# A decoder block with retrieved experts: two groups of four token tiles instead of three, with three dense tiles' gates made at the end of the second

## The chip, the cores and the metric

One core of a Trainium2 chip runs the whole block in one program. The metric is the device time of an execution in microseconds; a number given for a kernel is the median of its runs. TensorE is PE in the rows (its weight loads PEld), VectorE is DVE, ScalarE ACT, GpSimd POOL, and SyncE, which issues most transfers, SP. All arithmetic is in fp32.

## The reference

1024 tokens of width 1024 pass through one layer: a conditioned norm, a combined input projection (2304 columns), sliding-window attention and a short gated convolution, an output projection, then a retrieval layer that takes most of the time. Its core:

```python
q = (hf @ w_query).reshape(t, 8, 256)                       # 8 heads
s1 = einsum('thd,hnd->thn', q[..., :128], peer_keys1)       # 128 keys a half
s2 = einsum('thd,hnd->thn', q[..., 128:], peer_keys2)
v1, i1 = top_k(s1, 16);  v2, i2 = top_k(s2, 16)
sc, ci = top_k(v1[..., :, None] + v2[..., None, :], 16)     # over the 256 pairs
e1, e2 = i1[ci // 16], i2[ci % 16]
idx, gates = e1 * 128 + e2, softmax(sc)
a   = gelu(einsum('td,thkd->thk', hx, peer_u[idx]))         # peer_u, peer_v: 16384 x 1024
out = einsum('thk,thkd->td', gates * a, peer_v[idx])
```

So each token uses 8 x 16 of 16384 experts. The result is scaled, added to the residual stream and normed.

## The kernel before, in words

**Tiles and their two ways.** The tokens are eight tiles of 128 (0 to 7). For the tiles in `SPARSE` (2, 6, 7) the retrieval is computed with gathers: POOL issues indirect DMAs that fetch one row of U or V for 128 tokens at a time (L939, 256 rows a tile), and DVE multiplies and sums them (L960 for U, L967 for V). `ROWS` = (3, 7) says how many row buffers there are: three ahead of the dense stage and seven in it. For the tiles in `DENSE` (0, 1, 3, 4, 5) it is computed with matmuls over all experts, 128 blocks of 128 experts, weighted by a table of gates that is zero for the experts that a token doesn't use.

**The front stage** handles the tiles in `GROUPS`: [0, 1, 2], [3, 4, 5] and [6, 7]. One `Front.run` does a group: norm, 18 blocks of 128 columns of the input projection, attention and convolution between them, 8 blocks of the output projection, the second norm, 16 blocks of queries. A block is one `lin` (L257): a weight tile of 128 columns is the stationary operand, and the group's tokens, 128 wide a tile, move, so that a matmul is 384 or 256 wide. For precision weights and activations are split into a high half H and a low half L (fp32r), and a block is 24 matmuls: 8 slices of the depth in three products, H·H, H·L and L·H (L264 to L270). `Weights.load` fetches a weight block once for each group and splits it in two parts of four slices: ACT casts H (L223), POOL subtracts to get L (L224). The activations' halves of groups one and two lie in `hDH` and `hDL`, five tiles wide, which the dense stage reads later; a group's second norm writes them over those of the first. Group two starts at the third tile, since tile 2 isn't dense. Group three has its own, `hSH` and `hSL`.

After each query block come the scores against 128 keys (L622), and DVE takes the 16 largest with five instructions a tile (`top16`, L139; MAX8, FIND_INDEX8, MATCH_REPLACE8). Every second block, `pairs_head` (L645) forms the candidates of a head on POOL and takes their 16 largest. The vectors of the conditioning come from w_ada on DVE and PE (L733 to L751) in group one: the first third ahead of its projections, the rest beside them (`extra`). The first norm of a group is made during the queries of the group ahead of it (`after`, `norm_ahead`, `put_all`).

**Selection and gates.** `select` (L664) turns a tile's candidates into gates (softmax, L672 to L678) and two expert numbers a pair. `choose` (L890) does this for a gathered tile and makes its indices. `dense_gates1` (L796) does it for a dense tile and then builds that tile's gate table, four tokens at a time, which I call a quad: one DVE instruction compares the key numbers with the tokens' e1 and e2 (`oh`, 128 x 1024, L813); every third quad's e1 half is multiplied by the gates on ACT (four instructions, L822), the others' on POOL (L826); four PE matmuls give the table 128 x 128 of each token (`G`, L836), and ACT copies them to a staging tile (L837). A staging tile holds `TG` = 32 tokens; with its last quad ACT's queue writes it to `G_d` in DRAM (L839), in runs of `GB` x `TG` floats. There are two staging tiles and three of `oh`.

**What runs beside what.** `Beside` lets a generator advance at a rate per unit of the front stage's work. The gates of tiles 0 and 1 run beside group two and those of 3, 4 and 5 beside group three (`gates_of`), as do the gathers of tile 2 (`gather`). `RATE_G` and `RATE_F` hold the rates, separate for the projections ("p") and the queries ("q"). Ahead of the first norm of group three all gates of 0 and 1 are finished, and a staging tile serves as its buffer (`ahead_of_last`). In the front stage the order of the instructions on each engine is made by a scheduler from the program's order and its own estimates.

**The dense stage** (`dense_experts`, L1052) follows. A block of 128 experts has an A product (L1112; U's halves against the dense tiles' tokens, in two pieces of 384 and 256 columns, `DENSE_CH`), then ACT's gelu on it, DVE's weighing by the table `Gb` (L1129, read from `G_d` for two blocks at a time, L1065), its H (ACT, L1130) and L (DVE, `WL`, L1133). Four blocks make a set, and for each set there are ten V products (L1158; 12 matmuls of 512 columns each). The stage starts with four A products; then two or three V products alternate with one A. U and V are split beside it: `split_U` (ACT L1075, POOL L1079, with two buffers for `UL`) and `split_V` (ACT L1091, POOL L1095). Here the order on each engine is the program's own (`manual_schedule`):

```python
seq = [("A", b) for b in range(CB)]
for k in range(nk):
    vu = [("V", k, hf, t) for hf in range(2) for t in range(ND)]
    for q in range(CB):
        if k + 1 < nk:
            seq.append(("A", (k + 1) * CB + q))
        seq += vu[q * 2 * ND // CB : (q + 1) * 2 * ND // CB]
```

What is left of the gathers is spread over the stage, and the selections of tiles 6 and 7 (`chosen`) are put between its first steps (L1304).

Of the kernel before, what the change touches and what calls it, by code (L numbers as in the profile page):

```python
# [18 lines left out]
P = 128  # L19
# [12 lines left out]
SPARSE = [2, 6, 7]  # L32
DENSE = [0, 1, 3, 4, 5]
DENSE_CH = [(0, 3), (3, 2)]
GROUPS = [[0, 1, 2], [3, 4, 5], [6, 7]]
ND = len(DENSE)
WD = ND * P
TG = 32
# [46 lines left out]
def block_kernel(  # L85
# [31 lines left out]
    hDH = cst.tile([P, NC, WD], F32R, name="hDH")  # L117
    hDL = cst.tile([P, NC, WD], F32R, name="hDL")
# [34 lines left out]
    with ExitStack() as fctx:  # L153
# [82 lines left out]
        def fp_small(name):  # L236
            return cst.tile([P, 48], F32, tag="hc", name=name)

        class Front:
# [225 lines left out]
            def run(self, prev=0, extra=None, modulate1=None, after=None):  # L465
# [42 lines left out]
                for cb in range(4):  # L508
                    for kind in range(3):
                        blk = 6 + 3 * cb + kind  # L510
                        at = 3 * cb + kind
                        if nxt < n and at % 3 == 0:
                            pend = (nxt, self.att_scores(nxt, qo))
                            nxt += 1
# [27 lines left out]
                        if pend is not None and at % 3 == 2:  # L542
# [63 lines left out]
                for hs in range(16):  # L606
# [24 lines left out]
                    for j, i in enumerate(self.tiles):  # L631
                        if hs == 0:
                            tb[i] = sl_.tile([P, 2, 16, 8], BF16, tag="tb", name=f"tb{i}", bufs=ND)
# [11 lines left out]
        def pairs_head(i, h, tv):  # L645
# [3 lines left out]
            if h == 0:  # L649
                scv[i] = sl_.tile([P, 8, 16], F32, tag="scv", name=f"scv{i}", bufs=ND)  # L650
                ci[i] = sl_.tile([P, 8, 16], U32, tag="ci", name=f"ci{i}", bufs=ND)
# [112 lines left out]
        def ada_rest(fp, n):  # L764
# [6 lines left out]
            elif n in (6, 7):  # L771
                r = fp.tile([P, 512], F32, tag="adar", name=f"adar{n}", bufs=2)
                ada_row(fp, n, acc, r)
                nc.sync.dma_start(s2_d[:, hs], r[0:1, :])
            elif n in (8, 9):
                r = fp.tile([P, 512], F32, tag="adar", name=f"adar{n}", bufs=2)
# [9 lines left out]
            elif n >= 10:  # L786
                r = fp.tile([P, 512], F32, tag="adar", name=f"adar{n}", bufs=2)
# [4 lines left out]
        def dense_gates(gg, tiles):  # L792
            for i in tiles:
                yield from dense_gates1(gg, i)

        def dense_gates1(gg, i):  # L796
# [10 lines left out]
            for tg in range(P // TG):  # L807
                stg = gg.tile([P, NK, TG], F32, tag="stg", name=f"stg{i}_{tg}", bufs=2)
                for q in range(TG // 4):
# [10 lines left out]
                    if q % 3 == 2:  # L820
# [159 lines left out]
        def front(q, hH, hL):  # L980
# [3 lines left out]
            front(0, hDH[:, :, 0 : 3 * P], hDL[:, :, 0 : 3 * P]),  # L984
            front(1, hDH[:, :, 2 * P :], hDL[:, :, 2 * P :]),
# [6 lines left out]
        with tc.tile_pool(name="f0", bufs=1) as f0:  # L992
# [4 lines left out]
            hT = f0.tile([P, NC, P], F32, name="hT0")  # L997
# [16 lines left out]
        gates_of = Beside(dense_gates(gg, [0, 1]))  # L1014
        last = Front(GROUPS[2], [(0, 2)], None, None, "g2")

# [371 lines left out]
```

## Time and profile before

| | |
|---|---|
| median of 3 runs | 2893.73 us (2891.33 to 2896.70) |
| profiled execution | 2898.18 us, its span 2896.4 us |
| mean granted clock of PE in it | 0.96 |
| busy in the span | PE 92%, DVE 77%, POOL 66%, ACT 36% |
| chain that ended last | PE 60%: A (L1112) 28%, V (L1158) 27% |
| first V product of the dense stage | at 1122.78 us |

A span is one profiled execution from its first to its last instruction. Busy shares are averages over stages with different limits, so a change in one stage is judged by that stage's own rows. In the rows below a number behind "x" counts instructions, L is the line of the program that issued them, and what stands in square brackets or behind the last bar is the engine's idle time and the work that ended it.

### The profile page before, as it was taken

What the parts mean: (1) busy time and instruction counts of PE and PEld (TensorE: products, weight loads), DVE (VectorE), ACT (ScalarE), POOL (GpSimd) and SP (SyncE); (2) the same over time, 40 slices, a digit from 0 to 9 for tenths busy, and PEclk for the clock granted to TensorE, in tenths of its full rate; (3) what the DMA queues carried; (4) which work ended last, traced back from release to release, by engine and by line L of the source; (5) the groups of instructions that cost most, each with busy time, mean ns of one, the idle gap of its engine ahead of it and who ended that gap; (6) DMA issues with size and microseconds to landing.
All of it is one profiled execution on the core that took longest, in us unless ns stands there. A gap on an engine that the chain in (4) does not pass through costs nothing.

```text
span 2896.4 us, 44035 instructions
## 1 busy us (share of the span) xinstructions
PE 2676.4 (92%) x15358; PEld 2430.8 (84%) x15358; DVE 2234.3 (77%) x4693; ACT 1034.7 (36%) x2219; POOL 1907.0 (66%) x1894
## 2 busy tenths in 40 slices
PE   5999877998789887999999999999999999999997
PEld 4778776788668786999999889999999899999996
DVE  8835998659977787787777777777778777777776
ACT  3345445474356642222222322222222222222222
POOL 2435755557646665777777677777777777777771
PEclk9999888799899998999999999999999999999999
DMA  8535357674356856988989899988988898898884
GB/s 315 207 92 173 92 142 220 186 191 123 93 119 172 224 163 213 336 303 335 342 317 336 300 332 331 336 326 314 338 317 335 307 341 327 315 338 319 322 326 147
DMA packets 381979, 750.63 MB, mean 259 GB/s; under 512 B 188598, under 2 KB 194742, under 8 KB 381756
## 3 DMA queue, kind: packets, MB, share of 16 engines
q0 software_dynamic: 110592, 402.70, 37.8%
q1 hardware_dynamic: 107004, 303.16, 30.4%
q10 hardware_dynamic: 164160, 41.94, 6.7%
q8 instruction: 121, 1.98, 0.3%
q14 instruction: 102, 0.84, 0.1%
HBM read 695.79 MB, written 51.92 MB: 258 GB/s over the span
## 4 chain that ended last, share of the span: by engine, by line
PE 60%; DVE 4%; POOL 3%; issue 3%; DMA 1%; ACT 1%; another core or an unknown queue 0%; SPq 0%; POOLq 0%; DVEq 0%; ACTq 0%
PE A L1112 28%; PE V L1158 27%; PE G L836 2%; DVE oh L813 1%; POOL VL L1095 1%; PE lin_g2in L267 1%; POOL L L224 1%; PE lin_g2o L267 1%; POOL u L939 1%; PE lin_g2q L267 1%; POOL oh L826 0%; DMA xr<-x1d 0%; DMA raw<-in_w_query_dram 0%; POOL UL L1079 0%
## 5 line engine op out<-in xcount | busy, mean ns | idle before, releaser
L224 POOL TENSOR_TENSOR L<-raw,H 128x512 fp32r<-128x512 f32 x252 | 336.1, 1344 | 287.7 <-ACT H L223 200.2
L939 POOL DMA_INDIRECT u<-in_peer_u_dram,idx x384 | 364.9, 950 | 240.3 <-DVE u L960 93.6
L1158 PE MATMUL V<-VH,WH 128*128 128x512 f32 x1280 | 502.9, 393 | 14.2 <-DVE acc_d L1165 10.4
L939 POOL DMA_INDIRECT v<-in_peer_v_dram,idx x384 | 362.2, 943 | 211.1 <-DVE u L960 69.0
L1158 PE MATMUL V<-VH,WL 128*128 128x512 f32 x1280 | 500.7, 391 | 0.0
L967 DVE SCALAR_TENSOR_TENSOR acc<-v,wv,acc 128x1024 f32<-128x1024 f32 x381 | 489.5, 1285 | 13.5 <-DMA v<-in_peer_v_dram,idx 9.1
L1158 PE MATMUL V<-VL,WH 128*128 128x512 f32 x1280 | 499.1, 390 | 0.0
L960 DVE SCALAR_TENSOR_TENSOR u<-u,h 128x1024 f32<-128x1024 f32 x384 | 457.5, 1214 | 6.9 <-DMA u<-in_peer_u_dram,idx 4.3
L1117 ACT ACTIVATE A<-A 128x384 f32<-128x384 f32 (+1 forms) x256 | 107.7, 422 | 972.8 <-PE A L1112 777.2
L1112 PE MATMUL A<-hDH,UH 128*128 128x384 f32 (+1 forms) x2048 | 344.8, 311 | 19.2 <-ACT UH L1075 18.2
L1095 POOL TENSOR_TENSOR VL<-V,VH 128x512 fp32r<-128x512 f32 x256 | 331.6, 1308 | 35.1 <-ACT VH L1091 32.7
L1112 PE MATMUL A<-hDH,UL 128*128 128x384 f32 (+1 forms) x2048 | 340.3, 308 | 7.4 <-POOL UL L1079 7.4
L1112 PEld LDWEIGHTS A<-hDH,UH 128*128 128x128 f32 x2048 | 321.5, 190 | 30.0 <-ACT UH L1075 19.0
L1129 DVE TENSOR_TENSOR A<-A,Gb 128x384 f32<-128x384 f32 (+1 forms) x256 | 126.3, 497 | 280.5 <-ACT A L1117 213.8
L1112 PE MATMUL A<-hDL,UH 128*128 128x384 f32 (+1 forms) x2048 | 341.4, 309 | 0.0
L1079 POOL TENSOR_TENSOR UL<-U,UH 128x1024 fp32r<-128x1024 f32 x128 | 309.1, 2415 | 31.6 <-ACT UH L1075 29.3
L1112 PEld LDWEIGHTS A<-hDH,UL 128*128 128x128 f32 x2048 | 308.6, 188 | 8.6 <-POOL UL L1079 8.6
L1112 PEld LDWEIGHTS A<-hDL,UH 128*128 128x128 f32 x2048 | 311.3, 189 | 0.0
L1158 PEld LDWEIGHTS V<-VH,WH 128*128 128x128 f32 x1280 | 241.1, 188 | 64.3 <-DVE acc_d L1165 15.1
L1158 PEld LDWEIGHTS V<-VH,WL 128*128 128x128 f32 x1280 | 240.9, 188 | 52.5
L1158 PEld LDWEIGHTS V<-VL,WH 128*128 128x128 f32 x1280 | 241.4, 189 | 46.1
L1165 DVE TENSOR_TENSOR acc_d<-acc_d,V 128x512 f32<-128x512 f32 x310 | 211.8, 683 | 57.1 <-PE V L1158 53.1
(311 smaller groups left out, 4335.5 us busy)
## 6 DMA issues: line engine op xcount, KB each, us to landing
U<-in_peer_uT_dram SPq DMA_DIRECT2D x128, 512.0 KB
V<-in_peer_v_dram SPq DMA_DIRECT2D x256, 256.0 KB
G_d<-stg ACTq DMA_DIRECT2D x20, 2048.0 KB
Gb<-G_d SPq DMA_DIRECT2D x64, 640.0 KB
raw<-in_w_in_dram SPq DMA_DIRECT2D x54, 512.0 KB
wada<-in_w_ada_dram SPq DMA_DIRECT2D x48, 512.0 KB
raw<-in_w_query_dram SPq DMA_DIRECT2D x48, 512.0 KB
raw<-in_w_out_dram SPq DMA_DIRECT2D x24, 512.0 KB
```

Source lines behind the costliest of these rows:

```text
L224: nc.gpsimd.tensor_tensor(L, src, H.bitcast(F32), op=ALU.subtract)
L267: nc.tensor.matmul(ps[:, :w], wt[:, c, :], h[:, q * (NC // 2) + c, o : o + w], start=(k == 0), stop=(k == 3 * NC - 1),)
L939: nc.gpsimd.indirect_dma_start(out=t, out_offset=None, in_=peer_u if which == "u" else peer_v, in_offset=bass.IndirectOffsetOnAxis(ap=idx[ ...
L960: nc.vector.scalar_tensor_tensor(t, t, 1.0, h2[i], op0=ALU.mult, op1=ALU.mult, accum_out=av[i][:, j : j + 1])
L967: nc.vector.scalar_tensor_tensor(acc[i], t, wv[i][:, j : j + 1], acc[i], op0=ALU.mult, op1=ALU.add)
L1079: nc.gpsimd.tensor_tensor(L, Ur.pop(b), Up[b][0].bitcast(F32), op=ALU.subtract)
L1095: nc.gpsimd.tensor_tensor(L, Vr.pop(v), Vp[v][0].bitcast(F32), op=ALU.subtract)
L1112: nc.tensor.matmul(ps[:, : n * P], u[:, c, :], h[:, c, sl], start=(k == 0), stop=(k == 3 * NC - 1))
L1117: nc.scalar.activation(w, w, AF.Gelu)
L1129: nc.vector.tensor_tensor(w3, w3, g, op=ALU.mult)
L1158: nc.tensor.matmul(ps, w[:, ts_], v, start=(n == 0), stop=(n == 3 * CB - 1))
L1165: nc.vector.tensor_tensor(accs[0][:, t, hs], accs[0][:, t, hs], ps, op=ALU.add)
```

## The change

- Two groups: `GROUPS` = [0, 1, 2, 3] and [4, 5, 6, 7]. A projection matmul is 512 wide; each weight block is loaded and split twice, not three times. Group three, with its buffers and its staging-tile norm, goes.
- `SPARSE` is now 2, 3, 7 and `DENSE` 0, 1, 4, 5, 6, still three and five. `hDH` and `hDL` are six tiles wide, group two starts at the third (`SECOND` = 2), and the first norm of its first two tiles waits in `hT0`, which is two tiles wide.
- Attention of a tile is put at every second block of the input projection instead of every third.
- The gates of tiles 0 and 1 run beside group two, as before, followed by the selection of tile 3. The gates of tiles 4, 5 and 6 are written behind group two, with all multiplications by the gates on POOL (`beside` is False).
- Only tile 7's selection is left between the first steps of the dense stage.
- `TG` is 16: a staging tile has half the tokens, and a write to `G_d` has 2 x 16 floats a run in place of 2 x 32.
- Buffers: w_ada 4 instead of 6, the conditioning rows 1 instead of 2, `UL` 1 instead of 2, gather rows in the dense stage 6 instead of 7.

```diff
-SPARSE = [2, 6, 7]
-DENSE = [0, 1, 3, 4, 5]
+SPARSE = [2, 3, 7]
+DENSE = [0, 1, 4, 5, 6]
-GROUPS = [[0, 1, 2], [3, 4, 5], [6, 7]]
+GROUPS = [[0, 1, 2, 3], [4, 5, 6, 7]]
+SECOND = 2
-TG = 32
+TG = 16
-ROWS = (3, 7)
+ROWS = (3, 6)
-RATE_F = {("p", 1): 0.3, ("q", 1): 0.0, ("p", 2): 0.1, ("q", 2): 0.0}
-RATE_G = {("p", 1): 0.65, ("q", 1): 0.0, ("p", 2): 1.25, ("q", 2): 0.4}
+RATE_F = {"p": 0.2, "q": 0.1}
+RATE_G = {"p": 0.6, "q": 0.1}
...
-    hDH = cst.tile([P, NC, WD], F32R, name="hDH")
+    hDH = cst.tile([P, NC, (SECOND + 4) * P], F32R, name="hDH")
...
-                        if nxt < n and at % 3 == 0:
+                        if nxt < n and at % 2 == 0:
...
-                        if pend is not None and at % 3 == 2:
+                        if pend is not None and at % 2 == 1:
...
-                w = fp.tile([P, D], F32, tag="wada", name=f"wada{n}_{q}", bufs=6).rearrange("p (k f) -> p k f", k=2)
+                w = fp.tile([P, D], F32, tag="wada", name=f"wada{n}_{q}", bufs=4).rearrange("p (k f) -> p k f", k=2)
...
-                    if q % 3 == 2:
+                    if beside and (t0 // 4) % 3 == 2:
...
-            front(0, hDH[:, :, 0 : 3 * P], hDL[:, :, 0 : 3 * P]),
-            front(1, hDH[:, :, 2 * P :], hDL[:, :, 2 * P :]),
+            front(0, hDH[:, :, 0 : 4 * P], hDL[:, :, 0 : 4 * P]),
+            front(1, hDH[:, :, SECOND * P :], hDL[:, :, SECOND * P :]),
...
-            hT = f0.tile([P, NC, P], F32, name="hT0")
+            hT = f0.tile([P, NC, (4 - SECOND) * P], F32, name="hT0")
...
-        gates_of = Beside(dense_gates(gg, [0, 1]))
+        gates_of = Beside(chain(dense_gates(gg, [0, 1], True), choose(3)))
         with tc.tile_pool(name="f1", bufs=1, reuse_waits="tile") as f1:
             fronts[1].fp = f1
-            for kind, cost in fronts[1].run(prev=3, after=ahead_of_last):
-                gates_of.run(cost, RATE_G[kind, 1])
-                gather.run(cost, RATE_F[kind, 1])
-        gates_of = Beside(dense_gates(gg, [3, 4, 5]))
...
-        gates_of.rest()
-        chosen = chain(choose(6), choose(7))
+            for kind, cost in fronts[1].run(prev=4):
+                gates_of.run(cost, RATE_G[kind])
+                gather.run(cost, RATE_F[kind])
+            gates_of.rest()
+        for _ in dense_gates(gg, [4, 5, 6], False):
+            pass
+        chosen = choose(7)
...
-                L = dp.tile([P, NC, P], F32R, tag="UL", name=f"UL{b}", bufs=2)
+                L = dp.tile([P, NC, P], F32R, tag="UL", name=f"UL{b}")
```

How this moves instructions is seen best on two engines; a row gives the line, the operation, out<-in with the number of the buffer behind each name, the shape, and how often it is repeated. First PE, before, late in group three's queries (`lin_g2q`: a query block, `pk`: scores against the keys, `G`: a quad's table):

```order
L267 MATMUL lin_g2q_0_9895<-hSL,H_0_9798 128x256 x4
L267 MATMUL lin_g2q_0_9895<-hSH,L_0_9799 128x256 x4
L267 MATMUL lin_g2q_0_9895<-hSH,H_1_9802 128x256 x2
L836 MATMUL G_2_5_9834<-oh_84_9757 128x128 x4
L267 MATMUL lin_g2q_0_9895<-hSH,H_1_9802 128x256 x2
L267 MATMUL lin_g2q_0_9895<-hSL,H_1_9802 128x256 x4
L267 MATMUL lin_g2q_0_9895<-hSH,L_1_9803 128x256 x4
L622 MATMUL pkg_1_0_9841<-keyg_1_9792,qqsg_1_9794 128x128 x2
L267 MATMUL lin_g2q_0_9964<-hSH,H_0_9887 128x256 x4
L267 MATMUL lin_g2q_0_9964<-hSL,H_0_9887 128x256
L836 MATMUL G_2_6_9923<-oh_88_9831 128x128 x4
```

The quads' matmuls stand between those of the query blocks, four at a time. The same engine after the change, at the end of group two's queries (the lines have moved by two; `eT`: the turn of a dense tile's selection):

```order
L269 MATMUL lin_g1q_0_7926<-hDL,H_1_7851 128x512 x4
L269 MATMUL lin_g1q_0_7926<-hDH,L_1_7852 128x512 x4
L624 MATMUL pkg_14_0_7884<-keyg_14_7841,qqsg_14_7843 128x128 x4
L624 MATMUL pkg_15_0_7952<-keyg_15_7922,qqsg_15_7924 128x128 x4
L802 MATMUL eT_8080<-ident,e_8050 128x128
L802 MATMUL eT_8080<-ident,e_8065 128x128
L802 MATMUL eT_8080<-ident,gates_8026 128x128
L838 MATMUL G_0_0_8095<-oh_0_8089 128x128 x4
L838 MATMUL G_0_1_8104<-oh_4_8092 128x128 x4
```

No quad of tiles 4, 5 and 6 stands ahead of the last query block and its scores; all 96 follow, 32 a tile, each tile behind its three `eT` rows, and behind the 96th comes the first A product. Of the quads of tiles 0 and 1 none has moved out of group two.

Second, ACT before, filling a staging tile of 32 tokens (`stg`, eight copies) beside group three's output projection (`ss_g`: squares for the second norm):

```order
L822 ACTIVATE oh_52_9550<-oh_52_9550,gT_9241 128x128 x4
L837 COPY stg_1_9410<-G_1_3_9499 128x128x4
L837 COPY stg_1_9410<-G_1_4_9556 128x128x4
L578 ACTIVATE junk2g_6_0_9510,ss_g_8940<-x1g_8937 128x128
L837 COPY stg_1_9410<-G_1_5_9565 128x128x4
L578 ACTIVATE junk2g_6_1_9512,ss_g_8940<-x1g_8937 128x128
L837 COPY stg_1_9410<-G_1_6_9574 128x128x4
L837 COPY stg_1_9410<-G_1_7_9584 128x128x4
L839 DMA G_d<-stg_1_9410 128x64x64
```

Behind the eighth copy comes the write. ACT after the change, in the gates of tile 5:

```order
L839 COPY stg_0_8454<-G_0_0_8461 128x128x4
L839 COPY stg_0_8454<-G_0_1_8470 128x128x4
L839 COPY stg_0_8454<-G_0_2_8479 128x128x4
L839 COPY stg_0_8454<-G_0_3_8489 128x128x4
L841 DMA G_d<-stg_0_8454 128x64x32
L839 COPY stg_1_8485<-G_1_0_8499 128x128x4
L839 COPY stg_1_8485<-G_1_1_8508 128x128x4
L839 COPY stg_1_8485<-G_1_2_8517 128x128x4
L839 COPY stg_1_8485<-G_1_3_8527 128x128x4
L841 DMA G_d<-stg_1_8485 128x64x32
```

A write now follows every fourth copy, nothing else of ACT's stands between, and the copies change between two staging tiles as before.

## Rows read from the trace of the kernel before

**Rows 1.** Stages: us; busy us (instructions) PE, PEld, DVE, ACT, POOL; clock; DMA; GB/s.

```profile
45.00:331.00 286.00, 265.13 (x1429) 235.79 (x1427) 198.98 (x731) 140.93 (x330) 140.73 (x202) 0.93 0.48 159
331.00:716.00 385.00, 334.34 (x1884) 304.30 (x1883) 312.38 (x1000) 192.73 (x441) 221.20 (x293) 0.89 0.58 167
716.00:1060.00 344.00, 281.30 (x2015) 257.71 (x2015) 284.27 (x785) 182.84 (x447) 208.00 (x249) 0.92 0.59 154
1060.00:1123.00 63.00, 41.39 (x241) 40.26 (x242) 47.95 (x135) 21.78 (x37) 28.93 (x26) 0.84 0.36 118
1123.00:2896.00 1773.00, 1742.53 (x9744) 1582.69 (x9743) 1358.24 (x1991) 484.48 (x953) 1298.36 (x1097) 0.99 0.88 319
```

**Rows 2.** PE: projection matmuls, A and V (start us, us); conditioning matmuls by lines.

```profile
699.79 0.87 PE L267 MATMUL lin_g1q<-hDL,H 128*128 128x384 f32 x4
700.50 0.86 PE L267 MATMUL lin_g1q<-hDH,L 128*128 128x384 f32 x4
...
1158.53 6.99 PE A L1112 x48
1165.52 8.19 PE V L1158 x36
...
L743 PE MATMUL ada_c<-ones,adaacc 128*128 128x1 f32 x80 | 14.6, 303 | 32.5 <-DVE adaacc L735 32.5
```

**Rows 3.** By lines (busy us, mean ns; idle before, releaser): weight splits, queries, w_ada.

```profile
L224 POOL TENSOR_TENSOR L<-raw,H 128x512 fp32r<-128x512 f32 x252 | 336.1, 1344 | 287.7 <-ACT H L223 200.2
...
L267 PE MATMUL lin_g2q<-hSH,H 128*128 128x256 f32 x128 | 25.1, 313 | 3.5 <-ACT H L223 3.5
...
  DMA wada<-in_w_ada_dram: 1.0, 2
```

**Rows 4.** Quads: DVE's part by lines; PE's parts by time (start us, us).

```profile
L813 DVE TENSOR_TENSOR oh<-keyno,eT 128x1024 f32<-128x1024 f32 x160 | 190.7, 1216 | 54.5 <-PE G L836 46.3 <-POOL L L224 6.3 <-ACT eT L803 1.6
...
378.38 2.84 PE L836 MATMUL G<-oh 128*128 128x128 f32 x24
...
413.18 5.17 PE L836 MATMUL G<-oh 128*128 128x128 f32 x24 [4.11 <-ACT oh L822]
...
942.61 1.05 PE L836 MATMUL G<-oh 128*128 128x128 f32 x8
...
964.83 1.16 PE L836 MATMUL G<-oh 128*128 128x128 f32 x8 [0.30 <-POOL oh L826]
```

**Rows 5.** DMA queues over the span: packets, MB, share of 16 engines.

```profile
q0 software_dynamic: 110592, 402.70, 37.8%
q1 hardware_dynamic: 107004, 303.16, 30.4%
q10 hardware_dynamic: 164160, 41.94, 6.7%
```

**Rows 6.** The turn from group three to the dense stage, PE and DVE by time.

```profile
1057.90 0.71 PE L622 MATMUL pkg<-keyg,qqsg 128*128 128x128 f32 x4 [0.74 <-ACT qqsg L619]
...
1066.55 0.23 DVE L145 FIND_INDEX8 ci<-scv,cand 128x8 uint32<-128x80 f32 x1
...
1072.72 0.43 DVE L675 TENSOR_REDUCE gs<-gates 128x8 f32<-128x128 f32 x1 [5.94 <-ACT gates L673]
...
1076.32 0.89 DVE L1129 TENSOR_TENSOR A<-A,Gb 128x384 f32<-128x384 f32 x2
...
1093.66 0.89 DVE L1129 TENSOR_TENSOR A<-A,Gb 128x384 f32<-128x384 f32 x2
...
1122.78 0.50 PE L1158 MATMUL V<-VH,WH 128*128 128x512 f32 x1 [3.01 <-DVE WL L1133]
```

**Rows 7.** The low half of U on POOL, and A's last matmuls on PE.

```profile
1523.88 1.10 PE L1112 MATMUL A<-hDH,UL 128*128 128x256 f32 x8
...
1524.58 2.42 POOL L1079 TENSOR_TENSOR UL<-U,UH 128x1024 fp32r<-128x1024 f32 x1
```

**Rows 8.** By lines: DVE's sums over gathered rows of V.

```profile
L967 DVE SCALAR_TENSOR_TENSOR acc<-v,wv,acc 128x1024 f32<-128x1024 f32 x381 | 489.5, 1285 | 13.5 <-DMA v<-in_peer_v_dram,idx 9.1
```

More of the change, by code (lines that the diff above doesn't have):

```diff
@@ L236, in fp_small @@
         def fp_small(name):
-            return cst.tile([P, 48], F32, tag="hc", name=name)
+            return cst.tile([P, 64], F32, tag="hc", name=name)
         class Front:
@@ L632, in run @@
                         if hs == 0:
-                            tb[i] = sl_.tile([P, 2, 16, 8], BF16, tag="tb", name=f"tb{i}", bufs=ND)
+                            tb[i] = sl_.tile([P, 2, 16, 8], BF16, tag="tb", name=f"tb{i}", bufs=6)
                         if s == 0:
@@ L771, in ada_rest @@
             elif n in (6, 7):
-                r = fp.tile([P, 512], F32, tag="adar", name=f"adar{n}", bufs=2)
+                r = fp.tile([P, 512], F32, tag="adar", name=f"adar{n}", bufs=1)
                 ada_row(fp, n, acc, r)
@@ L775, in ada_rest @@
             elif n in (8, 9):
-                r = fp.tile([P, 512], F32, tag="adar", name=f"adar{n}", bufs=2)
+                r = fp.tile([P, 512], F32, tag="adar", name=f"adar{n}", bufs=1)
                 ada_row(fp, n, acc, r)
@@ L786, in ada_rest, with dense_gates, dense_gates1 @@
             elif n >= 10:
-                r = fp.tile([P, 512], F32, tag="adar", name=f"adar{n}", bufs=2)
+                r = fp.tile([P, 512], F32, tag="adar", name=f"adar{n}", bufs=1)
                 ada_row(fp, n, acc, r)
                 nc.sync.dma_start(g2_d[:, hs], r[0:1, :])
-        def dense_gates(gg, tiles):
+        def dense_gates(gg, tiles, beside):
             for i in tiles:
-                yield from dense_gates1(gg, i)
-        def dense_gates1(gg, i):
+                yield from dense_gates1(gg, i, beside)
+        def dense_gates1(gg, i, beside):
             e1, e2 = yield from select(i)
@@ L1013, in block_kernel @@
         gather = Beside(sparse_experts())
-        gates_of = Beside(dense_gates(gg, [0, 1]))
-        last = Front(GROUPS[2], [(0, 2)], None, None, "g2")
-        def ahead_of_last():
-            gates_of.rest()
-            st = gg.tile([P, NK, TG], F32, tag="stg", name="stg_x", bufs=2).rearrange("p a b -> p (a b)")
-            xb = st[:, 0 : 2 * D].rearrange("p (a d) -> p a d", d=D)
-            return norm_ahead(last, fronts[1], xb, st[:, 2 * D : 4 * D].rearrange("p (c t) -> p c t", c=NC))
+        gates_of = Beside(chain(dense_gates(gg, [0, 1], True), choose(3)))
         with tc.tile_pool(name="f1", bufs=1, reuse_waits="tile") as f1:
             fronts[1].fp = f1
-            for kind, cost in fronts[1].run(prev=3, after=ahead_of_last):
-                gates_of.run(cost, RATE_G[kind, 1])
-                gather.run(cost, RATE_F[kind, 1])
-        gates_of = Beside(dense_gates(gg, [3, 4, 5]))
-        with tc.tile_pool(name="f2", bufs=1, reuse_waits="tile") as f2:
-            last.hH = f2.tile([P, NC, 2 * P], F32R, name="hSH")
-            last.hL = f2.tile([P, NC, 2 * P], F32R, name="hSL")
-            last.fp = f2
-            last.put_all()
-            for kind, cost in last.run(prev=3):
-                gates_of.run(cost, RATE_G[kind, 2])
-                gather.run(cost, RATE_F[kind, 2])
-        gates_of.rest()
-        chosen = chain(choose(6), choose(7))
+            for kind, cost in fronts[1].run(prev=4):
[5 more added lines that the diff above has]
+        chosen = choose(7)
         pctx.close()
```

6 lines of the change are left out of this document (3 added, 3 removed).

## The prediction

> **What bounds the kernel now.** I read the table of stages first [rows 1]; its bounds are the first projection of each group, the first A product and the first V product, and its columns give each engine's busy time. The dense stage, 1123 to 2896 us, is 1773 us long, and PE is busy for 1742.5 of it at a clock of 0.99; DVE (1358), POOL (1298) and ACT (484) have room. The change leaves its matmuls alone, so it keeps its length, if its covers hold (below). The time is decided ahead of it: group one 286 us, group two 385, group three 344, and a turn of 63 us from there to the first V product. In these, PE is busy for 93, 87, 82 and 66%, DVE for 70, 81, 83 and 76%. No engine is full; PE and DVE take turns, and what counts is PE time left uncovered: 21, 51, 63 and 22 us, 156 in all. The change pays if its own uncovered time is less.
>
> Next, prices [rows 2]. A projection matmul of 384 columns starts every 176 ns (0.71 us for four). 24 of them and 24 of 256 make an A product of 6.99 us, so one of 256 is 115 ns. One of 512 is 227.5 ns (36 V matmuls in 8.19 us). A group has 18 + 8 + 16 blocks of 24 matmuls, 1008. All projections: before 1008 x (176 + 176 + 115) = 471 us, after 1008 x 2 x 227.5 = 459. So width alone gives 12 us of PE. Of the weight splits, 84 of 252 halves go, 113 us of POOL at 1344 ns each; but POOL is busy for only 57 and 60% of groups two and three, and PE waited for the high half of a query weight for 3.5 us in all of group three [rows 1, 3]: I cost their removal at nothing beyond the widths.
>
> **The fourth tile in groups one and two.** Its projections add 1008 x (227.5 - 176) = 52 us of PE to each. The rest goes by tile: group one's PE time is 265 us [rows 1], less 177 for projections, less 15 for the conditioning matmuls (L743) [rows 2], leaves 73 for three tiles, 24 each. So 76 a group, with the idle time kept as it is. Bounds: 52, if all the rest falls into idle PE, and 95 (286/3), if everything grows by tile. Group one then ends at 45 + 1.5 (one more tile to normalise, 0 to 4) + 286 + 76 = 408, group two (64 one-hot quads beside it, as before) at 408 + 385 + 76 = 869.
>
> **The gates at the end.** Before, 96 quads for three dense tiles stood beside group three; the change puts them behind the last projection, where PE has nothing else. Four steps:
> - DVE first finishes top-16 and candidates: before, 8.9 us from the last key product to the last index for two tiles [rows 6], so 9 to 18 for four; I take 14. Then the selection: for tile 6 it took 1072.72 to 1093.66, 20.9 us with four rows of A inside [rows 6], some 17 without; the new order puts first steps of the next tiles between, so 24. Together 38 (28 to 46).
> - The first quads fill a staging tile: a quad costs 1.2 us on DVE and 0.9 on PE; 16 of them, with little else on PE, ran in 23.4 us, 1.46 each [rows 4]. Four and the first's way through: 8 us.
> - 24 writes to G_d. The staging tile is halved and its runs go from 256 to 128 bytes, so each write has as many packets (8192, 512 for each of 16 engines) as one of the 20 writes before, for half the bytes. A packet of 256 bytes cost 0.067 x 16 x 2896 us / 164160 = 18.9 ns, one of q0 (3641 bytes) 158.4 ns [rows 5]: a line through both gives 8.4 ns and 0.0412 ns a byte, and 125 for q1 where 131.7 was measured. At 128 bytes: 13.7 ns, 7.0 us a write. Four quads at 1.46 take 5.8, so the writes pace the stage: there are two staging tiles, and ACT's copy waits for the write before last. 24 x 7.0 = 168 us. Bounds: 140, the quads alone (96 x 1.46), and 232 (24 x 9.7, a packet as dear as before).
> - Last write landed, two Gb reads of 640 KB, first weighing: 7 us (2 to 14; nothing shows it before, where the gates were done in time).
>
> The Trainium skill ("DMA: Bandwidth & Descriptors", Why small descriptors are slow) charges a packet its 32-byte beats and about 3 cycles; by that rule 128 bytes cost 7/11 of 256, an estimated 12.0 ns, and the sum would be 20 us shorter. I keep the line through the rows, which fits a third queue.
>
> **The turn.** Before, 46.5 us from the first weighing (1076.32) to the first V product (1122.78) [rows 6], with two selections on DVE in the way, for tiles 6 and 7; now there is one. The one that goes held DVE about as long as the other, some 17 to 20 us; PE still has three A products to issue there, so I count 10 of it: 36 us (26 to 46).
>
> **Sum.** 869 + 38 + 8 + 168 + 7 + 36 = 1126 us, where V starts at 1122.8 now: +4 us. The profiled execution (2898.18 us, span 2896.4) lies 4.5 above the median of 2893.73; on the median I forecast **2898 us**. That is no difference that a measurement of this kernel can tell (about 0.2%, 5.8 us).
>
> **Edits at nothing, and their cover.** UL in one buffer: POOL's next split starts at 1524.58, and A's last eight matmuls begin at 1523.88 and take 1.1 us [rows 7], so it would wait some 0.5 us; two or three V products (5.5 or 8.2 us) lie between A and the next. Without that cover it costs 2.4 us an A, 128 times. Six gather rows instead of seven: DVE waited 9.1 us for 381 rows of V in all [rows 8]. Gathers left for the dense stage: 735 by the order instead of 731. Four w_ada buffers: DVE waited 1.0 us for w_ada [rows 3]; a slower start would be seen in the first 45 us.
>
> **Rivals.**
> *A, small packets cost as much as large ones (slower).* Place: the 24 writes. Queued behind the ACT copy that waits for a staging tile are all later copies, hence PE's G products, hence DVE's next one-hots. From 7.1 us a write on, the time is slower than now by more than can be told; at 8.3 it is 2929, at 9.7 2962. For: these are the only small packets of any weight, and the rate of a still smaller one is not in this trace. Against: three queues lie on one line. Chance 0.22. The Trainium skill (same page, Specifications) says that below 512 bytes an engine reads, modifies and writes, which speaks against this change; the 256-byte packets here lie on the line, so no row bears it out.
> *B, the fourth tile fits into idle PE (faster).* For: groups one and two leave 72 us of PE uncovered, and attention of one tile can run beside projections of the others. Against: in the top-16 stretch DVE has about as much to do as PE. At 58 us a group instead of 76 the time is 2862. Chance 0.27.
> *C, the writes keep up (faster).* Then the quads' own 140 us pace the stage: 2870. For it packets must cost under 11.3 ns. Chance 0.10.
> *D, ACT stuck in group two (slower).* With four quads to a staging tile, a burst of quads there is held to 1.75 us each, and the weight casts queue behind the copies on ACT, so projections wait; also, one-hot products take 1.7 us a quad in some stretches instead of 0.9 (24 matmuls in 5.17 and in 2.84 us) [rows 4]. 64 x 0.3 to 0.55: 2917 to 2933. Chance 0.08.
> That the change would not do what it says I exclude: the order shows all 96 quads behind the last projection.
>
> **Numbers.** The forecast (2885 to 2912) has 0.33: of it 0.03 lies faster than can be told, 0.16 within, 0.14 slower. With the rivals: faster 0.03 + 0.27 + 0.10 = 0.40, within 0.16, slower 0.14 + 0.22 + 0.08 = 0.44. The range reaches from B, with some room below, to most of A: 2850 to 2955.
>
> **What would show it.** Projections of 512 columns at 227 to 230 ns; the first group's last key product near 408 us, the second's near 869; first G product of the last 96 near 907; q10 with about 328000 packets at 13.7 ns; a write issued every 7.0 us in the stage, ACT's copies waiting for a DMA; V from about 1126 us; then 1773 us with PE above 98%. The forecast is wrong if a write takes 8 us or more, if a group takes 20 us more or less than said, or if POOL's UL shows up in what A waits for.

## The result and the profile after

The change makes the kernel slower: 2932.02 us (median of 4 runs, 2930.66 to 2933.51) against 2895.22 for the kernel before in the same session, a ratio of 1.0127 (95% interval 1.0110 to 1.0145), +37 us. The forecast was 2898 us within 2850 to 2955. The profiled execution took 2933.51 us, its span 2930.9.

The page's chain that ended last (by engine, by line) and its row of the queue that carries the writes to `G_d`:

```profile
q10 hardware_dynamic: 328320, 41.95, 9.5%
...
PE 75%; DVE 13%; DMA 7%; ACT 2%; issue 2%; POOL 1%; ACTq 0%; SPq 0%; DVEq 0%; POOLq 0%
PE A L1099 29%; PE V L1145 28%; DMA G_d<-stg 4%; PE lin_g0in L269 3%; PE lin_g0q L269 3%; PE G L838 2%; PE lin_g0o L269 2%; PE lin_g1o L269 2%; DVE oh L815 2%; PE lin_g1in L269 1%; DVE u L962 1%; PE po L421 1%; DVE eq L720 1%; DVE ti L147 1%; DVE Skg L145 1%
```

The writes (`G_d<-stg`), which the page of before does not name in its chain, now hold 4% of the span in it, some 117 us. Their packets took 0.095 x 16 x 2930.9 / 328320 = 13.6 ns each, where 13.7 was forecast. The table of stages, with the columns of [rows 1]; its bounds are the first projection of each group, the start of the last key product, the first matmul of the last 96 quads, the end of the last of them and the first V product:

```profile
51.00:411.00 360.00, 340.25 (x1551) 258.84 (x1549) 226.90 (x909) 164.28 (x371) 152.38 (x226) 0.96 0.40 134
411.00:888.00 477.00, 412.65 (x1971) 325.10 (x1971) 359.52 (x1283) 207.07 (x476) 221.87 (x333) 0.90 0.54 130
888.00:920.00 32.00, 1.44 (x6) 0.58 (x4) 31.60 (x168) 2.98 (x6) 5.30 (x22) 0.54 0.00 1
920.00:1095.00 175.00, 120.47 (x774) 109.96 (x774) 132.18 (x153) 53.56 (x100) 104.52 (x96) 0.87 0.89 141
1095.00:1158.00 63.00, 41.80 (x234) 40.70 (x234) 25.92 (x58) 21.38 (x36) 23.81 (x14) 0.78 0.48 132
1158.00:2930.00 1772.00, 1747.92 (x9753) 1591.95 (x9751) 1356.62 (x1996) 484.32 (x951) 1303.59 (x1104) 0.99 0.88 321
```

Against [rows 1]: the dense stage kept its length (1772 us). Ahead of it, group three and the old turn (716.7 to 1122.8, 406 us) are gone; in their place stand 6 us at the start, 73 more in group one, 92 more in group two, and 271 us from the last key product to the first V product, in which PE is busy for 164. That makes +36. In the 175 us of the quads no engine is full, but the DMA engines are busy for 0.89 of it, and nearly all of that is the queue of the writes (0.87). ACT's timeline there (start us, us; ACTq is its queue, in brackets its idle time and what ended it):

```profile
1003.80 1.56 ACT L839 COPY stg<-G 128x512 f32<-128x512 f32 x3 [4.24 <-DMA G_d<-stg]
1005.69 0.59 ACT L839 COPY stg<-G 128x512 f32<-128x512 f32 x1 [0.33 <-PE G L838]
1006.31 3.35 ACTq L841 DMA_DIRECT2D G_d<-stg  x1
1010.99 1.56 ACT L839 COPY stg<-G 128x512 f32<-128x512 f32 x3 [4.71 <-DMA G_d<-stg]
1012.89 0.59 ACT L839 COPY stg<-G 128x512 f32<-128x512 f32 x1 [0.33 <-PE G L838]
1013.50 3.37 ACTq L841 DMA_DIRECT2D G_d<-stg  x1
```

Each staging tile's first copy waits for a write to land, and here a write is issued every 7.2 us (7.3 on the mean of the stage, stops between the tiles included). That is what a stage paced by its writes looks like, as forecast; e1 and e2 test it. Behind it comes the turn, here from SP, ACT, DVE and PE (first rows of SP: the two reads of the table, then V's loads; the last row is the first V product):

```profile
1107.10 0.80 SPq L1052 DMA_DIRECT2D Gb<-G_d  x2
1107.95 1.73 SPq L1071 DMA_DIRECT2D V<-in_peer_v_dram  x3
...
1114.60 0.62 ACT L1078 CAST VH<-V 128x512 fp32r<-128x512 f32 x1 [13.93 <-DMA V<-in_peer_v_dram]
1117.42 0.75 ACT L1104 ACTIVATE A<-A 128x384 f32<-128x384 f32 x2
1119.48 0.31 ACT L675 ACTIVATE gates<-gates 128x128 f32<-128x128 f32 x1
...
1119.82 0.38 DVE L677 TENSOR_REDUCE gs<-gates 128x8 f32<-128x128 f32 x1 [30.54 <-ACT gates L675]
1123.36 0.89 DVE L1116 TENSOR_TENSOR A<-A,Gb 128x384 f32<-128x384 f32 x2
1140.64 0.89 DVE L1116 TENSOR_TENSOR A<-A,Gb 128x384 f32<-128x384 f32 x2
...
1142.71 2.93 PE L1099 MATMUL A<-hDH,UH 128*128 128x384 f32 x8 [8.07 <-ACT UH L1062]
...
1158.83 0.40 PE L1145 MATMUL V<-VH,WH 128*128 128x512 f32 x1
```

The reads go out when the last write has landed (1107.1). V's loads stand behind them on SP, ACT's casts of V wait for the loads, and the first gelu stands behind the casts. DVE idles for 30.5 us, then does the selection of tile 7 in front of the first weighing (1123.36) and between it and the second (1140.64). ACT rounds the second's result before it casts the next block of U, and PE's fourth A product (1142.71) waits for that cast.

### The profile page after: what moved, and what is told of

The parts are those of the page before. It is cut to its first block, busy times and chain, and to the rows that moved or that the text cites. A ratio compares the mean times of both kernels' runs of the same rounds, so it can differ in the third digit from the quotient of the medians.

```text
span 2930.9 us, 41413 instructions
## 1 busy us (share of the span) xinstructions
PE 2677.3 (91%) x14334; PEld 2338.2 (80%) x14334; DVE 2168.1 (74%) x4620; ACT 947.3 (32%) x1960; POOL 1820.9 (62%) x1822
## 3 DMA queue, kind: packets, MB, share of 16 engines
q10 hardware_dynamic: 328320, 41.95, 9.5%
## 4 chain that ended last, share of the span: by engine, by line
PE 75%; DVE 13%; DMA 7%; ACT 2%; issue 2%; POOL 1%; ACTq 0%; SPq 0%; DVEq 0%; POOLq 0%
PE A L1099 29%; PE V L1145 28%; DMA G_d<-stg 4%; PE lin_g0in L269 3%; PE lin_g0q L269 3%; PE G L838 2%; PE lin_g0o L269 2%; PE lin_g1o L269 2%; DVE oh L815 2%; PE lin_g1in L269 1%; DVE u L962 1%; PE po L421 1%; DVE eq L720 1%; DVE ti L147 1%; DVE Skg L145 1%
## 5 line engine op out<-in xcount | busy, mean ns | idle before, releaser
L969 DVE SCALAR_TENSOR_TENSOR acc<-v,wv,acc 128x1024 f32<-128x1024 f32 x381 | 489.5, 1285 | 31.4 <-DMA v<-in_peer_v_dram,idx 26.8
L226 POOL TENSOR_TENSOR L<-raw,H 128x512 fp32r<-128x512 f32 x168 | 228.0, 1362 | 369.2 <-ACT H L225 208.1
L1082 POOL TENSOR_TENSOR VL<-V,VH 128x512 fp32r<-128x512 f32 x256 | 330.6, 1305 | 36.4 <-ACT VH L1078 34.1
L838 PE MATMUL G<-oh 128*128 128x128 f32 x1280 | 199.6, 317 | 86.0 <-POOL oh L828 42.4
## 6 DMA issues: line engine op xcount, KB each, us to landing
G_d<-stg ACTq DMA_DIRECT2D x40, 1024.0 KB, 11.8
```

The lines of the kernel that those rows point to most:

```text
L226: nc.gpsimd.tensor_tensor(L, src, H.bitcast(F32), op=ALU.subtract)
L838: nc.tensor.matmul(ps[:, :, k], oh2[:, k, :], og[:, k, :], start=True, stop=True)
L969: nc.vector.scalar_tensor_tensor(acc[i], t, wv[i][:, j : j + 1], acc[i], op0=ALU.mult, op1=ALU.add)
L1082: nc.gpsimd.tensor_tensor(L, Vr.pop(v), Vp[v][0].bitcast(F32), op=ALU.subtract)
```

## The experiments

All runs but e8 in one table; the columns in the middle are read from each trace (start of the last key product, issue of the last write to `G_d`, start of the first V product, and from there to the end of the span). Ratios are to the kernel before, run in the same session; runs without one were timed once.

| run | last key product | last write | first V | dense stage | median us | ratio (95%) |
|---|---|---|---|---|---|---|
| the change | 888.0 | 1095.8 | 1158.8 | 1772.1 | 2932.0 | 1.0127 (1.0110 to 1.0145) |
| e1_stage32 | 888.1 | 1061.7 | 1124.7 | 1772.2 | 2898.2 | 1.0012 (0.9995 to 1.0029) |
| e2_stage8 | 885.8 | 1211.1 | 1274.5 | 1772.4 | 3048.7 | |
| e3_v_first | 883.6 | 1091.1 | 1147.9 | 1772.9 | 2925.5 | 1.0111 (1.0075 to 1.0148) |
| e4_all_at_end | 792.1 | 1067.3 | 1130.9 | 1771.1 | 2903.8 | |
| e5_choose_ahead | 885.8 | 1098.2 | 1145.7 | 1773.4 | 2922.7 | 1.0100 (1.0074 to 1.0126) |
| e6_no_front_gathers | 862.7 | 1068.8 | 1132.6 | 1787.9 | 2923.3 | 1.0094 (1.0064 to 1.0124) |
| e7_together | 861.7 | 1049.9 | 1090.8 | 1791.8 | 2882.8 | 0.9950 (0.9938 to 0.9962) |
| e9_best_no_gathers | 864.9 | 1047.3 | 1088.1 | 1778.4 | 2870.4 | 0.9915 (0.9900 to 0.9931) |
| e10_best | 885.9 | 1073.7 | 1114.4 | 1770.3 | 2887.0 | 0.9974 (0.9963 to 0.9985) |
| e11_before_choose_ahead | | | 1124.0 | 1772.2 | 2898.1 | 1.0021 (1.0011 to 1.0032) |
| e12_tied | 859.7 | 1036.9 | 1080.4 | 1795.4 | 2877.9 | 0.9939 (0.9920 to 0.9958) |

**e1 and e2: do the writes pace the end?** Behind group two its space is free, so there the staging tiles can be of any size (`TG2` is 32 in e1 and 8 in e2):

```diff
+TG2 = 32
+TGS = [TG, TG, TG2, TG2, TG2]
...
-        for _ in dense_gates(gg, [4, 5, 6], False):
-            pass
+        with tc.tile_pool(name="g2", bufs=1, reuse_waits="tile") as g2:
+            late.append(g2)
+            for _ in dense_gates(gg, [4, 5, 6], False):
+                pass
```

(`G_d` holds each tile in runs of its own size, and the weighing reads them in three pieces instead of two.)

> The changed kernel, with one edit: tiles 4, 5 and 6 use staging tiles of 32 tokens, in space that group two leaves free, so that their 12 writes to G_d have runs of 256 bytes. Theory 1, the writes pace the end stage (one every 7.3 us for four quads, where the quads alone take 1.46 each): the writes fall to at most 9.7 us for eight quads, the quads' own 140 us pace the stage, the last write lands some 30 to 45 us earlier, and the time is 2885 to 2905. Theory 2, the quads are held by DVE, POOL and PE, and the writes only wait for them: within 5 us of 2932.

> As the kernel with staging tiles of 32, but with 8 tokens for tiles 4, 5 and 6: 48 writes with runs of 64 bytes, 8192 packets each. Theory 1 (the writes pace, a packet costs 8.4 ns and 0.041 ns a byte): 11.0 ns a packet, 5.6 us a write, 270 us for all, so some 100 us over the changed kernel, 3030. If a packet under 128 bytes costs as much as one of 128 (13.6 ns): 7.0 us a write, 334 us, 3100. Theory 2 (the writes don't pace): 2932.

Theory 1 holds both ways. In e1 the last write goes out 34.1 us earlier and the whole gain, 34 us, arrives at the end. ACT's copies wait there for a write to land for 5 us in all, against 76 in the change (ACT's waits in the stage: us in total, times, longest; the change, then e1):

```profile
ACT stg L839 <- DMA G_d<-stg: 76.0, 18, 6.5
```

```profile
ACT stg L843 <- DMA G_d<-stg: 5.2, 4, 1.8
```

ACT's queue in e1, then in e2:

```profile
1051.84 0.37 ACTq L845 DMA_DIRECT2D G_d<-stg  x1
1061.69 0.37 ACTq L845 DMA_DIRECT2D G_d<-stg  x1
```

```profile
1098.07 2.51 ACTq L845 DMA_DIRECT2D G_d<-stg  x1
1104.20 2.53 ACTq L845 DMA_DIRECT2D G_d<-stg  x1
```

In e1 a write comes every 9.85 us for eight quads, 1.23 each: that is DVE's one-hot (1.2 us), which now paces. From the first write to the last it is 124.7 us for 88 quads, 1.42 each with the stops between tiles; 1.46 was forecast. In e2 two quads take 6.1 us, and 48 such writes some 295, where the line of prices gave 270: the time lies 117 us above the change, and some 100 were expected.

**e3: what holds the first weighing?**

```diff
+        for _ in range(VRAW):
+            fetch_next()
         for j in range(2):
             load_G(j)
-        for _ in range(VRAW):
-            fetch_next()
```

> The changed kernel, with the first three loads of V issued on SP ahead of the first two reads of the gate table instead of behind them. Theory 1: those reads wait for the last write to G_d and hold the loads behind them, ACT's casts of V wait for the loads, and the first gelu, queued behind the casts, is late; so the first weighing comes 5 to 10 us earlier, and with it the first V product and the end: 2922 to 2927. Rival: the first weighing waits for the table itself and for the selection of tile 7 ahead of it on DVE, so nothing comes earlier: 2932 within 3 us.

SP's reads of the table and DVE's first weighing in e3:

```profile
1102.51 0.80 SPq L1052 DMA_DIRECT2D Gb<-G_d  x2
...
1112.90 0.89 DVE L1116 TENSOR_TENSOR A<-A,Gb 128x384 f32<-128x384 f32 x2
```

From the last write's landing to the first weighing it took 10.4 us instead of 16.3, and from the last write's issue to the first V product 56.8 instead of 63.0. So V's loads behind the table's reads were worth 6 us. The ratio fell by only 0.0016, inside its interval, so the gain is shown by the trace and not by the times.

**e5: the selection of tile 7.** All its steps come before the dense stage's first:

```diff
     with tc.manual_schedule(engines=ORDERED):
+        for _ in chosen:
+            pass
         for n, cost in enumerate(dense_experts()):
-            for _ in range(0 if n < 1 or n > 8 else 2 if n < 8 else 9):
-                next(chosen, None)
```

> The changed kernel, with the whole selection of tile 7 put ahead of the dense stage's first step instead of between its first steps. In the changed kernel DVE idles for 30 us from the last one-hot (1089.3) to that selection's second step (1119.8), and then holds A's first two weighings back by 3.7 and 13.5 us. Theory 1, the selection on DVE sets the turn: it falls into the idle stretch, the second weighing follows the first at once, and the first V product comes 10 to 18 us earlier: 2914 to 2922. Rival: the turn is set by PE's A products at the low clock and by the loads of U, and V comes at most 4 us earlier: 2928 to 2932.

Theory 1 holds for the turn: last write to first V 47.5 us instead of 63.0. The time, 2922.7, is just above the range of theory 1 and below that of the rival: the scheduler put the selection among the quads, and from the last key product to the last write it took 212.4 us instead of 207.8. DVE in e5, from the last one-hot on, where the second weighing follows the first within 4 us:

```profile
1093.04 1.22 DVE L815 TENSOR_TENSOR oh<-keyno,eT 128x1024 f32<-128x1024 f32 x1 [0.48 <-PE G L838]
1120.63 0.90 DVE L1116 TENSOR_TENSOR A<-A,Gb 128x384 f32<-128x384 f32 x2 [26.36 <-ACT A L1104]
...
1124.38 0.90 DVE L1116 TENSOR_TENSOR A<-A,Gb 128x384 f32<-128x384 f32 x2
```

**e11: the same edit in the kernel before**, as a control.

> The kernel before, with its two selections (tiles 6 and 7) put ahead of the dense stage's first step. There DVE has no idle stretch at the turn (5.9 us at most). Theory 1, the gain of this edit in the changed kernel comes from DVE's idle time while the last writes run: here the selections only move ahead of the first weighing, and the time is 2890 to 2905. Rival, the order of selections and weighings costs time in both kernels: 2880 to 2886.

It is 0.2% slower, inside the range of theory 1: there DVE idles for 5.9 us at most at the turn, and the selections only move ahead of the first weighing (1099.4 instead of 1076.3). So the gain belongs to the wait for the last writes, which the change made.

**e4: what does a quad cost beside group two?** All 160 quads behind it, on top of e1:

```diff
-TGS = [TG, TG, TG2, TG2, TG2]
+TGS = [TG2] * 5
...
-        gates_of = Beside(chain(dense_gates(gg, [0, 1], True), choose(3)))
+        gates_of = Beside(choose(3))
```

> As the kernel with staging tiles of 32, and the gates of tiles 0 and 1 are made at the end too: no quad runs beside group two, 160 behind it. It measures what 64 quads cost beside group two (477 us in the changed kernel, with 80 us of PE time in them and 29 of waiting for them). Theory A, a quad costs PE as much beside as alone: group two falls by some 95 to 110 us, the end stage grows by 64 x 1.46 = 93, and the time is that of the kernel with staging tiles of 32 within 15 us. Theory B, the quads fill time in which PE idles anyway: group two falls by 50 at most, and the time is 40 or more above it.

Theory A, within a few us: group two is 93 us shorter (408.2 to 792.1), 1.45 a quad, the end 102 longer, 1.6 a quad, and the time is 5.5 us above e1's. Beside the projections a quad is hardly cheaper than alone.

**e6: the gathers beside group two.**

```diff
-                gather.run(cost, RATE_F[kind])
+                if gather.done < 7:
+                    gather.run(cost, RATE_F[kind])
```

> The changed kernel, with the gathers beside group two cut to the selection of tile 2 and the first row; the other 32 rows go to the dense stage. Group two's input projections take 271 us, and without any quad beside them still 233, against 177 in group one, with 41 us in which PE waits, 30 of them for DVE's part of the attention. Theory 1, the gathered rows on DVE (33 of 1.2 us) hold the attention back: group two falls by 20 to 35 us, the dense stage stays at 1772, and the time is 2897 to 2912. Rival: the quads' one-hots and the selections are what holds DVE, and group two falls by at most 10: 2922 to 2932. If the dense stage pays for the rows (DVE is busy for 77% of it), it gets longer by what they cost, up to 40 us.

Group two's input projections in the change, in e6, and in the kernel before (columns of [rows 1]):

```profile
411.00:682.00 271.00, 217.90 (x967) 162.84 (x966) 214.65 (x559) 108.28 (x250) 119.52 (x132) 0.86 0.58 144
```

```profile
410.00:654.00 244.00, 212.43 (x967) 158.57 (x966) 182.31 (x495) 100.97 (x243) 89.11 (x101) 0.88 0.43 93
```

```profile
331.00:537.00 206.00, 169.91 (x876) 145.17 (x875) 174.60 (x423) 88.82 (x202) 108.36 (x110) 0.86 0.57 169
```

PE waits there for 53 us in the change, 32 without the rows, and 36 before. So the rows do hold PE up, and the stage falls by 27 us, as in theory 1. That they do so through DVE is likely (the attention's part of PE's wait is ended by DVE) but not shown: e6 takes the issues of the gathers off POOL as well, which is busy for 89 us there instead of 120. And the time misses theory 1's range: the dense stage pays 16 us back, and the time falls by some 10 (by the ratio, whose interval overlaps that of the change). The expectation said 233 us for this stage in e4, from a window that reached into the output projections; its own length there is 211, with 39 us of waiting, 37 of them in the attention.

**e7, e9, e10 and e12: together.** e7 is e1, e3, e5 and e6 in one:

> Four edits at once: staging tiles of 32 tokens at the end, V's loads ahead of the table's reads, the selection of tile 7 ahead of the dense stage, no gathered rows beside group two. If each does what it did or is expected to do alone and they don't overlap: 2932 - 34 - 7 - 12 - 20 = 2859, and the kernel beats both. Where two edits remove the same wait the sum is smaller; if the selection and the gathers don't matter, 2890.

It beats the kernel before by 0.5%, 24 us short of the sum. Two reasons stand in its rows: the dense stage is 20 us longer, and the selection of tile 7 slipped in among the quads, since the order before the dense stage is the scheduler's. From the first quad's matmuls to the end of the last's it takes 155 us instead of e1's 141. In e9 its large part takes its scratch tiles from the one-hot buffers and so can't start before the last quads; e10 is the same with the gathered rows left beside group two; e12 ties the small steps too.

```diff
+        def eq_oh(name):
+            t = gg.tile([P, 2, 4, NK], F32, tag="oh", name=name, bufs=3)
+            return t.rearrange("p a b c -> p (a b c)")[:, 0:512].bitcast(BF16).rearrange("p (a b) -> p a b", a=16)
+
+        for _ in choose(7, eq_oh):
+            pass
```

> As the four edits at once, but the last and largest part of tile 7's selection (13.5 us on DVE) is tied to the one-hot buffers, so that it comes behind the last one-hot, in DVE's idle stretch, and not among the quads, where it made the end stage 16 us longer (157 us instead of 141). If the quads are then paced by DVE's one-hots again: the end stage takes 141 us, the turn stays at 41, and the time is 2883 - 16 = 2867, faster than both kernels. Rival: the selection only moves from the quads into the turn: 2880 to 2885.

> The same with the gathered rows left beside group two, as in the changed kernel. Without them group two was 27 us shorter and the dense stage 16 to 20 longer, so this one is 7 to 11 us slower than the one without: 2874 to 2878 if that one is at 2867. If the dense stage's extra time there has another cause than the rows, it is the faster of the two.

> As the fastest kernel so far (2870, no gathered rows beside group two), with the small steps of tile 7's selection (ten instructions from the copy of its candidates' numbers on) tied to the one-hot buffers too. There they stood among the quads, where such an instruction takes some 1.06 us if POOL's multiplication runs, against 0.23 alone. If that is the price of their place: ten times 0.8, so the last quad comes some 8 us earlier, the selection still fits into DVE's wait for the table (7 us of it were left), and the time is 2860 to 2866. Rival: the place of the small steps costs nothing, since the quads wait for PE and POOL as long: 2868 to 2873.

By the medians e9 is the fastest kernel of the study: 2870.4 us, 0.85% under the kernel before, 2.1% under the change. DVE in e9 at the turn: the selection's last step, then a wait for the table alone:

```profile
1055.38 0.29 DVE L902 SCALAR_TENSOR_TENSOR idx<-e,e 128x128 int32<-128x128 f32 x1
1062.62 1.10 DVE L1134 TENSOR_TENSOR A<-A,Gb 128x256 f32<-128x256 f32 x3 [6.95 <-DMA Gb<-G_d]
```

But it did not gain as expected: from the last key product to the last write it is 182.4 us against 188.2 in e7, so 6 of the expected 16 came back, the first V product is 2.7 earlier, and the other 13 lie in the dense stage (1778.4 against 1791.8). In e12 the same stretch is 177.2, 5 shorter again (8 expected), V starts 7.7 earlier than in e9, and the dense stage takes more than that back: 1795.4. The time, 2877.9, lies above the ranges of both theories, though the ratios of e9 and e12 overlap. In the kernels with the rows left beside group two that stage takes 1770 to 1776 in every trace; without them 1778 to 1795. PE's V products by line, over the whole span, in e10 and in e12, show part of it:

```profile
L1162 PE MATMUL V<-VH,WH 128*128 128x512 f32 x1280 | 500.2, 391 | 7.5 <-DVE acc_d L1169 7.5
```

```profile
L1164 PE MATMUL V<-VH,WH 128*128 128x512 f32 x1280 | 505.5, 395 | 18.4 <-DVE acc_d L1171 16.5 <-DVE acc_d L1169 1.1
```

V waits longer for DVE's sums (`acc_d`), which free its PSUM tiles: 18.4 us against 7.5, and 16.6, 18.6 and 10.8 in e6, e7 and e9. That is some 10 us of the 25. That DVE, busy for 79% of the stage instead of 77%, comes late more often because of the added rows is not shown: e9's DVE is the busiest of all (80%), and e9 loses least. What lengthens the stage stays open. e10 is 17 us slower than e9 by the medians (7 to 11 expected): the rows cost 26 us ahead of the first V product, and e9's dense stage pays back only 8.

**e8: the start.**

> The changed kernel, with six buffers for w_ada as before, paid for with one buffer less for each of three other kinds of tile (raw weights, attention's turned tiles, the groups' temporaries), which slows what follows; only the first 55 us are to be read. Theory 1, four buffers make DVE wait for w_ada: the first projection starts at 45 to 48 us, as before the change (45.8), instead of 51.9. Rival, the fourth tile's norm makes it late: it starts at 50 to 52.

```profile
L269 PE MATMUL lin_g0in<-hDH,H x144: 388/396/797, 48.0 to 232.6; 128*128 128x512 f32 x144
```

The first projection (first start in this row of its line) is at 48.0 instead of 51.9; the run's time, 2973.9 us, was expected to suffer from the three buffers taken away and is not read. So some 4 of the 6 us are the two buffers of w_ada (one run; the other kernels with four buffers start it at 51.9 to 53.7). Some 2 are left for the fourth tile and the conditioning rows in one buffer, which no run tells apart.

## Why the prediction was right in the main and 33 us short in its sum

The range holds the measured time; the point forecast, no difference that can be told, was wrong: the kernel is slower, clear of the noise. By the prediction's own terms, each to the next point of time:

| term | forecast | measured |
|---|---|---|
| first projection | 46.5 | 51.9 |
| group one | 361.5 | 359.1 |
| group two | 461 | 477.0 |
| lead, and first staging tile (to the first of the 24 writes) | 46 | 39.6 |
| first write's issue to last landing | 168 | 179.5 |
| to the first weighing | 7 | 16.3 |
| turn | 36 | 35.5 |
| first V product | 1126 | 1158.8 |
| dense stage | 1773.6 | 1772.1 |

**Right.** The dense stage kept its length, with `UL` in one buffer (A waited for it for 4.7 us, 7.4 before) and six rows (DVE waited for rows of V for 26.8 us instead of 9.1, and PE did not feel it). The fourth tile cost group one 73 us where 76 was said. The writes pace the end stage (e1, e2), at the packet price that the line through [rows 5] gave (13.6 ns, 13.7 forecast); without them the quads pace it at the forecast 1.4 to 1.5 us. In the turn one selection was left at a price of some 10 us: in e5, without it, the turn takes 25.1 us (1120.63 to 1145.7) instead of 35.5.

The 73 us were luck in part. Two rows of PE in group two's queries, four matmuls of 512 columns each:

```profile
841.26 1.09 PE L269 MATMUL lin_g1q<-hDL,H 128*128 128x512 f32 x4
842.19 1.09 PE L269 MATMUL lin_g1q<-hDH,L 128*128 128x512 f32 x4
```

So a projection matmul starts every 233 ns, and not every 227 to 230; the 227.5 came from V's matmuls. A group's projections are 5 us dearer for it, the other work of the fourth tile came out as much cheaper, and of the 12 us of PE that the width was to save some 2 are left.

**Wrong**, by 33 us in sum, and nearly all on one side:
- *Group two, "with the idle time kept as it is": +16.* PE's busy time came out as forecast (412.7 against 410). Its waits did not stay at 51 us, they grew to 64, all in the input projections (36 to 53). By PE's rows the waits for quads grew there from 19 to 26 us and those of the attention from 10.5 to 22.4, with four tiles instead of three. Group one, with neither quads nor rows beside it, kept its waits (20 us). So idle time that comes with each tile's attention has to be scaled with the tiles where the engines have other work. That the gathered rows are part of this work e6 shows: without them the waits fall to 32 us. Attention also stands at every second block now instead of every third, and no run tells that from the number of tiles. The text's upper bound, everything by tile (95), was nearer.
- *24 writes, 7.0 each: +11.5.* They came every 7.31 us (23 intervals in 168.2). Two are in flight at a time, so that a write takes longer from issue to landing than from one issue to the next (11.8 us on the median), and the last landed 11.3 us after its issue: the sum left out a queue's last turn.
- *"Last write landed ... first weighing: 7": +9.* The term looked at the table's way alone. On SP, V's loads are queued behind its reads, on ACT the gelu behind V's casts, on DVE the weighing behind a selection whose first step waits for ACT. e3 took 6 us out of this stretch. e5 took 15.5 out of this stretch and the turn, some 6 of them here.
- *The start, "0 to 4" for one more tile: +5.* The loads of w_ada had been watched ("a slower start would be seen"), but at no price; e8 shows some 4 us for them. The 1.0 us of waiting that the prediction read is that of one of two lines; both together waited 3.9 us before and 7.4 after.
- *The lead: -6*, inside its bounds.

The rows behind the first of these, PE's waits for DVE's part of the attention in group two's input projections (us in total, times, longest), before and after; the rest of the 22.4 us is one wait of 5.9 for an ACT copy of the attention:

```profile
PE pT L414 <- DVE Ss L400: 8.5, 2, 4.9
PE S L361 <- DVE mx L371: 1.9, 1, 1.9
```

```profile
PE pT L416 <- DVE Ss L402: 13.7, 4, 8.2
PE S L363 <- DVE mx L373: 2.7, 1, 2.7
```

**The rivals.** The time is what rival A gives at 8.3 us a write (2929), yet that is a coincidence and A is not what happened: a write took 7.3, and only 11.5 of the 33 us are its. That "three queues lie on one line" was weak evidence against A: two of them drew the line, so that the 256-byte packets lie on it by construction, and the third lay 5% off; 13.6 ns at 128 bytes is the first real test of it. D names the right place, group two, and a like size, but the wrong wait: PE's quads waited for ACT's staging copies for only 5.5 us in its input projections. B fell too: it needed 58 us a group, and the fourth tile cost 73 and 92. What C describes, quads that pace the stage, is what e1 shows with runs of 256 bytes.

The Trainium skill ("DMA: Bandwidth & Descriptors", Why small descriptors are slow) counts 32-byte beats and some 3 cycles a packet; from 18.9 ns at 256 bytes that is an estimated 12.0 at 128 and 8.6 at 64. The runs show 13.6 at 128 (read from the page of the profile, as the 18.9 were) and 12.0 at 64 (a write every 6.1 us in e2, 512 packets an engine): the fixed part is larger than by that rule. The Trainium skill (same page, Specifications) lets one expect a step up in price below 512 bytes. Between 256, 128 and 64 bytes the price only falls; no queue of these runs has packets between 256 bytes and a mean of some 2830 (q1 in [rows 5]), so whether a step lies there no run shows.

## What to carry to other kernels

A stage moved to where nothing else runs gets a new bound, and its own waits no cover: look at its transfers, its first and its last step, before counting its engines. Scale a stage's idle time with the work that made it, instead of keeping it as it is. An earlier start of the next stage is not yet an earlier end: e6 and e12 gave back in the dense stage what they had gained ahead of it, or most of it. And where work goes into an engine's idle stretch, tie it there by a buffer, if a scheduler sets the order.

## What the runs showed of the hardware

Some small DVE instructions wait for POOL. In e7, where the selection stands among the quads, DVE and POOL by time:

```profile
962.48 0.21 DVE L688 TENSOR_SCALAR t<-cu 128x128 uint32<-128x128 uint32 x1
...
963.90 1.15 POOL L832 TENSOR_TENSOR oh<-oh,gT 128x512 f32<-128x512 f32 x1 [0.23 <-DVE oh L819]
964.08 1.06 DVE L689 TENSOR_SCALAR t<-t 128x128 uint32<-128x128 uint32 x1
```

The first takes 0.21 us while POOL waits; the like one that starts in POOL's multiplication ends just after it, after 1.06. The Trainium skill ("SBUF — State Buffer", Terms) speaks of a port pair that the two share, held for a whole instruction, the other one blocked; the rows agree. Not all are held: the one-hots themselves, one of whose operands lies in PSUM, kept their 1.2 us beside the same multiplications.
